# State-space part: decay products over 128 rows, per-head scalars on ScalarE, the attention half of w_out loaded beside the attention

## The chip, the cores and the metric

The kernel runs on one core of a Trainium2 chip. The metric is device time in microseconds (us) of one execution. A core has five engines with queues of their own: TensorE (PE) multiplies matrices, VectorE (DVE) and ScalarE (ACT) work on tiles from SBUF and PSUM, GpSimd (POOL) on tiles from SBUF, and SyncE (SP) issues the transfers to and from memory here. Each takes its instructions in the order in which they were written down for it; semaphores hold an instruction until what it reads is there and what it overwrites is no longer needed.

## What is computed

One encoder layer over 1024 tokens of width 1024: a half-step feed-forward network (FFN), a mixing layer, a second FFN and a gated embedding, each followed by a LayerNorm. The mixing layer has two halves: attention with 8 heads, and a bidirectional state-space scan (SSD) with 8 heads of 64 channels, 2 groups and 128 states. Their outputs, side by side, are multiplied by `w_out`. The scan is computed in chunks of 128 tokens, in both directions:

```python
a_cum = jnp.cumsum(adt, axis=-1)
seg = a_cum[..., :, None] - a_cum[..., None, :]
Lmat = jnp.exp(jnp.where(tril, seg, -jnp.inf))
cb = jnp.einsum('bclgn,bcsgn->bcgls', c_c, b_c)
y_diag = jnp.einsum('bcgls,bgrcls,bcsgrp->bclgrp', cb, Lmat, xd)
decay_states = jnp.exp(a_cum[..., -1:] - a_cum)
states = jnp.einsum('bcsgn,bgrcs,bcsgrp->bcgrpn', b_c, decay_states, xd)
...
def step(h, inp):
    st, d = inp
    return h * d[..., None, None] + st, h
...
y_off = jnp.einsum('bclgn,bcgrpn,bgrcl->bclgrp', c_c, prev, jnp.exp(a_cum))
...
y = y_f + y_b + d_skip[i].astype(jnp.float32).reshape(G, R)[:, :, None] * xh
y = y.reshape(B, S, SSD_WIDTH) * jax.nn.silu(z.astype(jnp.float32))
...
mix = jnp.concatenate([att_out, ssd_out], axis=-1) @ w_out[i]
```

## The kernel before, in words

Large products are taken in three parts: each fp32 operand is split into a high part (a cast on ScalarE, L100 `split_into`) and a low part (a subtraction on VectorE, L82 `lo`), and `mm3` (L114) sums high x low, low x high and high x high.

The order of the stages is: first FFN, projections of q, k, v, z, x, B, C and the step sizes, attention, the scan from right to left (`ssd_right`, L1160), the scan from left to right (`ssd_left`, L1230), second FFN, gate. PE runs its instructions in program order (`in_order`). On the other engines a scheduler places each instruction when the program is built, by its own estimate of times; the order that results is fixed.

`ssd_tables` (L1136) builds tables for the decay products before the attention starts: `LT` holds in 27 of 59 rows per direction three ones and three bf16 parts of eight heads' sums, `RT` (two buffers, one for even and one for odd chunks) the matching rows for the other side, `mask` the triangle, `idb` the identity.

`ssd_right` goes through chunks 7 to 0. For a chunk, `front` takes the decay matrix of each direction as products into a PSUM tile `big` (two such tiles): for each half of the heads the identity times the mask (L1183), then 27 rows of `LT` times 27 rows of `RT` (L1184). ScalarE's exponential (L1186) turns the tile into `Ef` or `Eb`. B times C goes to PSUM (L1190) and is copied to `cb` (L1192). One step later `mid` forms the skip term `y` on GpSimd (L1197), and on VectorE the sum of both directions (L1198) and its product with `cb` (L1201). `offdiag` (L1108) multiplies the running state into PSUM (L1112), scales it by head on VectorE (L1114, `toff`) and adds it to `y` on GpSimd in this pass (L1115). `next_state` (L1117) scales the chunk's input by head on GpSimd (L1120, `xs`), multiplies (L1123), scales the old state by head on GpSimd (L1128) and adds (L1129; for the first chunk L1126 copies). Two steps later `back` multiplies the decay matrix with the input (L1207), adds on VectorE (L1208) and stores `y` to `yd`. A product "by head" reads eight scalars per row, each spread over 64 columns.

Work of other kinds is put between the chunks as "fillers", called with the number of the step. In `ssd_right` these are `weights(0)` at step 1, which loads four raw tiles of the attention half of `w_out` and splits them into eight blocks `blk`, and `spilled(t)` at steps 4, 6 and 8, which multiplies one tile of 128 tokens of the attention output by it (`out_proj`, 24 matmuls of L114) and stores the result for later. In `ssd_left` they are the remaining tiles (`resident`), `weights(1)` and the tiles' second half with the LayerNorm (`mixed`).

`ssd_left` goes through chunks 0 to 7: `offdiag` (the addition on VectorE) and `next_state` for the other direction, then the product with `zs` on GpSimd (L1268), squares on ScalarE (L1272), the root on GpSimd (L128) with a correction on VectorE (L121 to L124), the scaling (L1278), and two chunks later a transpose on PE (L1251) into `mixT`, the split operand of the output projection. `mixT` takes four pairs of the buffers `xh00`, `xl00` to `xh11`, `xl11`: in each pair of halves the first number is the token half, the second 0 for the attention and 1 for the scan. Before that the same buffers held the layer's input of the projections.

## Time and profile before

| | us |
|---|---|
| median of 3 runs | 2109.38 (2101.42 to 2111.34) |
| the profiled execution | 2104.84 |
| span of its instructions | 2103.1 |
| first decay product of `ssd_right` | at 1132.91 |
| first product of `ssd_left` (L1123) | at 1208.85 |

The granted TensorE clock was 0.987 of full speed over the span. The profile gives times from the span's start. In a row of a timeline the first number is the start, the second the time taken, both in us; what stands in brackets is how long the engine had been idle and what ended that. In a row of groups the number behind `x` is the count, then total us and mean ns. The stages around the change, with the busy time of PE, weight loads, VectorE, ScalarE and GpSimd in us, then granted clock, share of the DMA engines and GB/s:

```profile
700.00:800.00 100.00, 100.00 (x474) 82.74 (x473) 56.80 (x130) 24.60 (x41) 16.35 (x9) 1.00 0.18 67
...
1050.00:1100.00 50.00, 50.00 (x302) 43.09 (x301) 46.87 (x64) 41.91 (x77) 4.87 (x6) 1.00 0.00 1
...
1200.00:1225.00 25.00, 23.76 (x107) 19.62 (x106) 9.20 (x15) 1.82 (x8) 11.04 (x10) 0.93 0.75 273
```

The first row lies in the z projection, where the tables are begun, the second in the attention, the third where `ssd_right` ends and `ssd_left` begins.

### The profile page before, as it was taken

What the parts mean: (1) busy time and instruction counts of PE and PEld (TensorE: products, weight loads), DVE (VectorE), ACT (ScalarE), POOL (GpSimd) and SP (SyncE); (2) the same over time, 40 slices, a digit from 0 to 9 for tenths busy, and PEclk for the clock granted to TensorE, in tenths of its full rate; (3) what the DMA queues carried; (4) which work ended last, traced back from release to release, by engine and by line L of the source; (5) the groups of instructions that cost most, each with busy time, mean ns of one, the idle gap of its engine ahead of it and who ended that gap; (6) DMA issues with size and microseconds to landing.
All of it is one profiled execution on the core that took longest, in us unless ns stands there. A gap on an engine that the chain in (4) does not pass through costs nothing. (4 is left out here: it accounts for less than half of the span.)

```text
span 2103.1 us, 25439 instructions
## 1 busy us (share of the span) xinstructions
PE 2024.0 (96%) x9316; PEld 1647.8 (78%) x9316; DVE 1571.8 (75%) x2339; ACT 806.1 (38%) x1324; POOL 678.4 (32%) x483
## 2 busy tenths in 40 slices
PE   7899999999999999999999998899999999999998
PEld 6688888887787888777886777688888888877886
DVE  6865665648899747658998679786666666889987
ACT  5433333335341224538886122333333334533121
POOL 0644444426530112000013542164444444541111
PEclk9999999999999999999999999999999999999999
DMA  7323433457531311220004372133333328642222
GB/s 258 114 100 121 164 116 122 149 177 273 180 111 60 117 39 37 76 74 11 1 1 144 114 270 80 71 110 122 139 130 144 128 101 323 204 133 91 71 81 80
DMA packets 94761, 254.33 MB, mean 121 GB/s; under 512 B 11585, under 2 KB 24257, under 8 KB 94636
## 3 DMA queue, kind: packets, MB, share of 16 engines
q1 hardware_dynamic: 92332, 248.51, 33.8%
q10 hardware_dynamic: 2304, 4.20, 0.5%
q8 instruction: 73, 1.20, 0.2%
q14 instruction: 52, 0.43, 0.1%
HBM read 184.84 MB, written 67.83 MB: 120 GB/s over the span
## 5 line engine op out<-in xcount | busy, mean ns | idle before, releaser
L114 PE MATMUL sm<-xh,blk 128*128 128x512 f32 x1440 | 453.5, 396 | 0.0
L114 PEld LDWEIGHTS sm<-xh,blk 128*128 128x128 f32 x1440 | 272.2, 189 | 64.7
L114 PE MATMUL sm<-xl,blk 128*128 128x512 f32 x720 | 286.2, 398 | 2.5 <-DVE xl L82 2.5
L114 PE MATMUL sm<-blk,xh 128*128 128x512 f32 (+2 forms) x912 | 277.3, 382 | 1.6 <-DVE rs_t L122 1.2
L114 PE MATMUL sm<-xl,xh 128*128 128x512 f32 x960 | 232.8, 393 | 8.0 <-DVE acc L352 7.3
L100 ACT CAST blk<-raw 128x512 fp32r<-128x512 f32 (+1 forms) x176 | 105.3, 611 | 333.6 <-PE sm L114 177.4
L114 PEld LDWEIGHTS sm<-xl,xh 128*128 128x128 f32 x960 | 178.4, 188 | 51.3 <-DVE acc L352 14.9
L82 DVE TENSOR_TENSOR blk<-raw,blk 128x512 fp32r<-128x512 f32 (+1 forms) x176 | 160.6, 923 | 58.4 <-ACT blk L100 57.7
L82 DVE TENSOR_TENSOR blk<-s,blk 128x512 fp32r<-128x512 f32 x176 | 149.0, 851 | 65.8 <-ACT blk L100 64.3
L114 PEld LDWEIGHTS sm<-blk,xh 128*128 128x128 f32 x912 | 169.7, 191 | 33.9 <-issue 1.4
L114 PE MATMUL big<-xl,xh 128*128 128x512 f32 x768 | 182.0, 394 | 6.4 <-DVE M L409 2.7
L114 PEld LDWEIGHTS big<-xl,xh 128*128 128x128 f32 x768 | 146.1, 191 | 38.2 <-ACT xl L388 5.7
L114 PE MATMUL sm<-blk,xl 128*128 128x512 f32 (+2 forms) x456 | 172.4, 378 | 0.0
L100 ACT CAST blk<-s 128x512 fp32r<-128x512 f32 x176 | 108.1, 621 | 159.9 <-PE sm L114 148.6
L114 PEld LDWEIGHTS sm<-xl,blk 128*128 128x128 f32 x720 | 136.1, 189 | 36.2 <-DVE xl L82 4.1
L244 POOL TENSOR_TENSOR s<-raw 128x512 f32<-128x512 f32 x42 | 56.0, 1332 | 291.2 <-DVE blk L82 205.8
L177 POOL TENSOR_TENSOR ln_k<-ln_k,mhalf 128x1 f32<-128x1 f32 x32 | 41.4, 1294 | 310.1 <-DVE ln_k L176 310.1
L114 PE MATMUL sm<-xET3h,blk 128*128 128x512 f32 x352 | 110.6, 395 | 0.2 <-DVE blk L82 0.2
L114 PE MATMUL sm<-xET2h,blk 128*128 128x512 f32 x352 | 110.7, 395 | 0.0
L327 POOL TENSOR_TENSOR u<-u,p 128x512 f32<-128x512 f32 x44 | 74.7, 1697 | 80.5 <-DVE u L326 80.5
L247 POOL TENSOR_TENSOR s<-raw,s 128x512 f32<-128x512 f32 x42 | 58.1, 1384 | 131.7 <-DVE blk L82 131.5
L114 PEld LDWEIGHTS sm<-blk,xl 128*128 128x128 f32 x456 | 87.2, 191 | 15.4
(303 smaller groups left out, 4046.5 us busy)
## 6 DMA issues: line engine op xcount, KB each, us to landing
raw<-in_wi_dram SPq DMA_DIRECT2D x84, 512.0 KB
hD<-sg SPq DMA_DIRECT2D x44, 512.0 KB
blk<-hD SPq DMA_DIRECT2D x44, 512.0 KB
wr<-in_wo_dram SPq DMA_DIRECT2D x32, 512.0 KB
wT<-wT SPq DMA_DIRECT2D x32, 512.0 KB
blk<-in_wo_dram SPq DMA_DIRECT2D x28, 512.0 KB
wT<-wt SPq DMA_DIRECT2D x32, 256.0 KB
wT<-wr SPq DMA_DIRECT2D x32, 256.0 KB
```

The lines of the kernel that those rows point to most:

```text
L82: (eng or self.nc.vector).tensor_tensor(out=out, in0=full, in1=hi.bitcast(F32), op=ALU.subtract)
L100: self.nc.scalar.copy(out=b[:, 0, :n], in_=src)
L114: self.nc.tensor.matmul(ps, lhsT=a, rhs=b, start=(i == 0), stop=(i == n - 1))
L177: nc.gpsimd.tensor_tensor(out=r, in0=v, in1=self.mhalf[:, :1], op=ALU.pow)
L244: G.tensor_tensor(out=s1, in0=a21, in1=a22, op=ALU.add)
L247: G.tensor_tensor(out=s4, in0=a12, in1=s2, op=ALU.subtract)
L327: G.tensor_tensor(out=u2, in0=u2, in1=p5, op=ALU.add)
```

## The change

1. The decay products take all 128 rows: `LT` becomes one zero-filled tile per direction, `RT` is zero-filled to 128 rows, and the rest of their rows stays zero, so the products are the same. The zero-fill (and the ones) moves to GpSimd; the constant rows are loaded in two halves.
2. Every GpSimd product by head (skip term, `xs`, old state) becomes eight ScalarE activations of 64 columns with a scalar per row (`scale_heads`). The addition in `offdiag` is on VectorE for both directions, and so is the product with `zs`. GpSimd keeps the roots.
3. The attention half of `w_out` is loaded in raw form into `xh01` and `xl01` right after the tables, while the attention runs, and split just before `ssd_right`. `mixT` gets its scan halves only after that, when the raw tiles have been read. The raw ring is no longer used for this half.
4. The three spilled tiles move from steps 4, 6 and 8 to steps 0, 1 and 8.

```diff
+    def scale_heads(self, out, src, small):
+
+        for h in range(8):
+            o = slice(h * HD, (h + 1) * HD)
+            self.nc.scalar.activation(out=out[:, o], in_=src[:, o], func=AF.Identity, scale=small[:, h:h + 1])
+
     def offdiag(self, pool, state, d, ch, bc, y):
...
-        (nc.gpsimd if d else nc.vector).tensor_tensor(out=y, in0=y, in1=t_, op=ALU.add)
+        nc.vector.tensor_tensor(out=y, in0=y, in1=t_, op=ALU.add)
 
     def next_state(self, pool, state, d, ch, xb):
...
-        G.tensor_tensor(out=self.heads(xs), in0=self.heads(xb[:, :512]), in1=self.per_head(self.sdt[:, ch, d * 8:d * 8 + 8]), op=ALU.mult)
+        self.scale_heads(xs, xb, self.sdt[:, ch, d * 8:d * 8 + 8])
...
-            G.tensor_tensor(out=self.heads(new), in0=self.heads(state), in1=self.per_head(self.cd[:, ch, d * 8:d * 8 + 8]), op=ALU.mult)
+            self.scale_heads(new, state, self.cd[:, ch, d * 8:d * 8 + 8])
...
     def ssd_tables(self, pool):
...
-        self.LT = LT = pool.tile([59, NT, P], BF16, name="LT")
-        self.RT = [pool.tile([59, 8, P], BF16, name=f"RT{b}") for b in range(2)]
+        self.LT = LT = [pool.tile([P, NT, P], BF16, name=f"LT{d}") for d in range(2)]
+        self.RT = [pool.tile([P, 8, P], BF16, name=f"RT{b}") for b in range(2)]
...
-        V.memset(LT, 1.0)
         for d in range(2):
+            G.memset(LT[d], 0.0)
+            G.memset(LT[d][32 * d:32 * d + 3], 1.0)
...
         for b in range(2):
-            V.tensor_copy(self.RT[1 - b], rraw)
+            G.memset(self.RT[b], 0.0)
+        for n in range(2):
+            hs = slice(4 * n, 4 * n + 4)
+            rraw = pool.tile([59, 4, P], F32, name="rraw")
+            nc.sync.dma_start(out=rraw, in_=I["rows"][:, hs])
+            for b in range(2):
+                V.tensor_copy(self.RT[b][:59, hs], rraw)
...
-                    nc.tensor.matmul(o, lhsT=LT[32 * d:32 * d + 27, ch], rhs=rt[32 * d:32 * d + 27, n * 4:n * 4 + 4], start=False, stop=True)
+                    nc.tensor.matmul(o, lhsT=LT[d][:, ch], rhs=rt[:, n * 4:n * 4 + 4], start=False, stop=True)
...
-            G.tensor_tensor(out=self.heads(y), in0=self.heads(xb[:, :512]), in1=self.per_head(dsk), op=ALU.mult)
+            self.scale_heads(y, xb, dsk)
...
-            G.tensor_tensor(out=y, in0=y, in1=zs, op=ALU.mult)
+            V.tensor_tensor(out=y, in0=y, in1=zs, op=ALU.mult)
...
-            mixT = self.new_xT()
             self.ssd_tables(tables)
+            early = []
+            for n in ("xh01", "xl01"):
+                r = self.xp.tile([P, 4, 512], F32, name=n).rearrange("p (a b) c -> p a (b c)", b=2)
+                for i in range(2):
+                    nc.sync.dma_start(out=r[:, i], in_=I["wm"][len(early)])
+                    early.append(r[:, i])
+            mixT = [[self.unit(h, 0)] for h in range(2)]
             with ExitStack() as c2:
                 self.attention(c2, mixT)
...
-            wm[half].extend(self.wload(I["wm"][half * 4 + k]) for k in range(4))
+            if half:
+                wm[1].extend(self.wload(I["wm"][4 + k]) for k in range(4))
+            else:
+                wm[0].extend([self.split(r[:, i * 512:(i + 1) * 512]) for i in range(2)] for r in early)
...
-            self.ssd_right(c, loaded, {1: lambda: weights(0), 4: lambda: spilled(0), 6: lambda: spilled(1), 8: lambda: spilled(2)})
+            weights(0)
+            for h in range(2):
+                mixT[h].append(self.unit(h, 1))
+            self.ssd_right(c, loaded, {i: lambda t=t: spilled(t) for t, i in enumerate((0, 1, 8))})
```

How the instructions stand now. ScalarE at the start of the right pass, from its last copy of the attention (`a_tmp`) on, before (`blk<-raw` is a split of w_out, `Ef` and `Eb` the exponentials, `cb` the copy of B times C):

```order
L1056 COPY a_tmp<-sm 64x512 x2
L1186 ACTIVATE Ef<-big 128x1024
L100 CAST blk<-raw 128x512
L1186 ACTIVATE Eb<-big 128x1024
L100 CAST blk<-raw 128x512
L1186 ACTIVATE Ef<-big 128x1024
L100 CAST blk<-raw 128x512 x2
L1186 ACTIVATE Eb<-big 128x1024
L1192 COPY cb<-sm 128x256 x2
```

And in the change (`y<-xb,dsk` is the skip term, `xs` the scaled input):

```order
L1056 COPY a_tmp<-sm 64x512 x2
L100 CAST blk<-xh_7569 128x512 x4
L100 CAST blk<-xl_7572 128x512 x4
L1200 ACTIVATE Ef<-big 128x1024
L1200 ACTIVATE Eb<-big 128x1024
L1206 COPY cb<-sm 128x256
L1112 ACTIVATE y<-xb,dsk 128x64 x8
L1112 ACTIVATE xs<-xb,sdt 128x64 x8
L1112 ACTIVATE y<-xb,dsk 128x64 x8
L1112 ACTIVATE xs<-xb,sdt 128x64 x4
L1200 ACTIVATE Ef<-big 128x1024
```

All eight splits now stand ahead of the first exponential, and the products by head stand between the exponentials.

ScalarE at the end of the right pass, before (`ysq` are the squares of the left pass):

```order
L1186 ACTIVATE Ef<-big 128x1024
L1186 ACTIVATE Eb<-big 128x1024
L1192 COPY cb<-sm 128x256
L1272 ACTIVATE ysq,yss<-y_10110 128x256 x2
L1272 ACTIVATE ysq,yss<-y_10114 128x256 x2
```

And in the change, from the next to last state of the pass to the left pass's first squares:

```order
L1112 ACTIVATE state<-state,cd 128x64 x8
L1112 ACTIVATE y<-xb,dsk 128x64 x5
L1112 ACTIVATE xs<-xb,sdt 128x64 x7
L1112 ACTIVATE state<-state,cd 128x64 x8
L1200 ACTIVATE Ef<-big 128x1024
L1112 ACTIVATE y<-xb,dsk 128x64 x8
L1200 ACTIVATE Eb<-big 128x1024
L1206 COPY cb<-sm 128x256
L1112 ACTIVATE xs<-xb,sdt 128x64 x24
L1112 ACTIVATE state<-state,cd 128x64 x8
L1112 ACTIVATE xs<-xb,sdt 128x64 x8
L1286 ACTIVATE ysq,yss<-y_10265 128x256 x2
```

The last state product of the right pass stands ahead of the last two exponentials; forty products by head of the left pass stand ahead of its first squares.

VectorE at the start of the right pass in the change (`a_raw` is the attention's output, `accr` the spilled tile):

```order
L1057 TENSOR_TENSOR a_raw<-sm,a_tmp 64x512 x2
L82 TENSOR_TENSOR blk<-xh_7569,blk 128x512
L1072 TENSOR_TENSOR a_raw<-a_raw,sm 128x512
L82 TENSOR_TENSOR blk<-xh_7569,blk 128x512 x3
L82 TENSOR_TENSOR blk<-xl_7572,blk 128x512 x4
L1212 TENSOR_TENSOR Eb<-Eb,Ef 128x1024
L1215 TENSOR_TENSOR Eb<-Eb,cb 128x512 x2
L1307 SCALAR_TENSOR_TENSOR accr<-sm,accr 128x512 x2
L1132 COPY state<-sm 128x512
```

There the sum of the two directions stood between the splits before; now the splits come first, and the first spilled tile's additions ahead of the first state.

More of the change, by code (lines that the diff above doesn't have):

```diff
@@ L1114, in offdiag @@
         nc.vector.tensor_tensor(out=self.heads(t_), in0=self.heads(po), in1=self.per_head(self.eF[:, ch, d * 8:d * 8 + 8]), op=ALU.mult)
[L1115 removed]
+        nc.vector.tensor_tensor(out=y, in0=y, in1=t_, op=ALU.add)
     def next_state(self, pool, state, d, ch, xb):
[L1118 removed]
+        nc = self.nc
         xs = pool.tile([P, 512], F32, name="xs")
[L1120 removed]
+        self.scale_heads(xs, xb, self.sdt[:, ch, d * 8:d * 8 + 8])
         pS = self.pss()
@@ L1138, in ssd_tables @@
         nc, I, V = self.nc, self.I, self.nc.vector
-        self.LT = LT = pool.tile([59, NT, P], BF16, name="LT")
-        self.RT = [pool.tile([59, 8, P], BF16, name=f"RT{b}") for b in range(2)]
+        G = nc.gpsimd
+        self.LT = LT = [pool.tile([P, NT, P], BF16, name=f"LT{d}") for d in range(2)]
+        self.RT = [pool.tile([P, 8, P], BF16, name=f"RT{b}") for b in range(2)]
         self.mask = pool.tile([P, 2, P], BF16, name="mask")
         self.idb = pool.tile([P, P], BF16, name="idb")
-        rraw = pool.tile([59, 8, P], F32, name="rraw")
-        nc.sync.dma_start(out=rraw, in_=I["rows"])
         mraw = pool.tile([P, 2, P], F32, name="mraw")
         nc.sync.dma_start(out=mraw, in_=I["mask"])
-        V.memset(LT, 1.0)
         for d in range(2):
+            G.memset(LT[d], 0.0)
+            G.memset(LT[d][32 * d:32 * d + 3], 1.0)
             for i in range(3):
-                nc.sync.dma_start(out=LT[32 * d + 3 + 8 * i:32 * d + 11 + 8 * i], in_=self.sc[1][d, i].rearrange("c h l -> h c l"))
+                nc.sync.dma_start(out=LT[d][32 * d + 3 + 8 * i:32 * d + 11 + 8 * i], in_=self.sc[1][d, i].rearrange("c h l -> h c l"))
         for b in range(2):
-            V.tensor_copy(self.RT[1 - b], rraw)
+            G.memset(self.RT[b], 0.0)
[5 more added lines that the diff above has]
+                V.tensor_copy(self.RT[b][:59, hs], rraw)
+        for b in range(2):
             self.rows(NT - 1 - b)
@@ L1162, in ssd_right @@
         nc, tc = self.nc, self.tc
-        V, G = nc.vector, nc.gpsimd
+        V = nc.vector
         ep = c.enter_context(tc.tile_pool(name="sexp", bufs=2))
@@ L1232, in ssd_left @@
         nc, tc = self.nc, self.tc
-        V, G = nc.vector, nc.gpsimd
+        V = nc.vector
         two = c.enter_context(tc.tile_pool(name="lwork", bufs=2))
```

1 line of the change is left out of this document (removed).

## The prediction

> **What bounds the kernel now.** I read the page first, then a table of stretches around the changed stages, then TensorE's timeline there, then the groups of the other engines.
>
> ```profile
> PE 2024.0 (96%) x9316; PEld 1647.8 (78%) x9316; DVE 1571.8 (75%) x2339; ACT 806.1 (38%) x1324; POOL 678.4 (32%) x483
> ```
>
> TensorE (PE) is busy 96% of the span.
>
> ```profile
> 1125.00:1150.00 25.00, 20.04 (x91) 12.34 (x89) 18.87 (x21) 14.39 (x25) 14.56 (x12) 0.89 0.78 255
> ...
> 1175.00:1200.00 25.00, 25.00 (x144) 19.34 (x142) 18.00 (x21) 5.65 (x8) 10.46 (x8) 1.00 0.24 82
> ...
> 1250.00:1275.00 25.00, 23.37 (x108) 18.98 (x107) 23.09 (x52) 6.56 (x19) 9.83 (x9) 1.00 0.43 148
> 1275.00:1300.00 25.00, 21.19 (x99) 17.29 (x98) 23.57 (x55) 4.42 (x10) 7.03 (x6) 0.93 0.16 63
> ```
>
> In these rows the columns after the length are busy us of PE, weight loads, VectorE (DVE), ScalarE (ACT), GpSimd (POOL), then the granted clock. The right-to-left pass (1133 to 1208) is bound by PE once it runs; ScalarE does 5.65 of 25 us there. The left-to-right pass and the start of the second FFN, up to 1356, share the bound between PE and VectorE, which is busy 92 to 94% from 1250 to 1300.
>
> ```profile
> 1132.22 0.58 ACT L1056 COPY a_tmp<-sm 64x512 f32<-64x512 f32 x1 [3.10 <-PE sm L1050]
> ...
> 1132.91 0.38 PE L1183 MATMUL big<-mask,idb 128*128 128x512 bf16 x1
> ...
> 1148.29 2.04 PE L1112 MATMUL sm<-state,bc 128*128 128x256 f32 x4 [4.82 <-DVE state L1126]
> ...
> 1153.32 0.38 PE L1183 MATMUL big<-mask,idb 128*128 128x512 bf16 x1
> ...
> 1155.86 0.71 PE L1190 MATMUL sm<-bc 128*128 128x128 f32 x4
> 1156.41 1.03 PE L1112 MATMUL sm<-state,bc 128*128 128x256 f32 x4
> 1157.27 1.03 PE L1123 MATMUL sm<-xs,xb 128*128 128x256 f32 x4
> 1158.13 1.90 PE L1207 MATMUL sm<-xb,Eb 128*128 128x64 f32 x16
> 1159.87 0.38 PE L1183 MATMUL big<-mask,idb 128*128 128x512 bf16 x1
> ...
> 1166.39 0.48 PE L114 MATMUL sm<-blk,xh 128*128 128x512 f32 x1
> ...
> 1172.08 0.39 PE L1183 MATMUL big<-mask,idb 128*128 128x512 bf16 x1
> ...
> 1208.85 1.62 PE L1123 MATMUL sm<-xs,xb 128*128 128x256 f32 x4 [1.24 <-POOL xs L1120]
> ...
> 1229.13 0.41 PE L1251 MATMUL sm<-ident,y 128*128 128x128 f32 x2 [2.95 <-DVE y L1278]
> ...
> 1281.44 1.09 PE L1251 MATMUL sm<-ident,y 128*128 128x128 f32 x4 [3.81 <-DVE y L1278]
> ```
>
> One chunk of the right pass takes PE 6.55 us (1153.32 to 1159.87): decay products 2.54, the rest 0.55, 0.86, 0.86 and 1.74. One tile of the attention half of the output projection takes 5.69 (1166.39 to 1172.08). The pass, from the first decay product at 1132.91 to the left pass's first product at 1208.85, is 75.9 us with two real waits: 4.82 for the first state, late behind the splits of w_out on VectorE, and 1.24 for `xs` on GpSimd.
>
> **The decay products over 128 rows.**
>
> ```profile
> PEld L1184 <- issue: 7.9, 32, 0.4
> PEld L1183 <- issue: 6.1, 26, 0.3
> ...
> 1166.94 0.63 PE L114 MATMUL sm<-blk,xh 128*128 128x512 f32 x2
> 1167.40 0.40 PE L114 MATMUL sm<-blk,xl 128*128 128x512 f32 x1
> ```
>
> A decay matmul starts 0.32 us after the one before (2.54/8), a 512-wide matmul of L114 0.23 (two in 0.46). The weight loads of the former wait out the running matmul; the 128-row loads of L114 do not. If the 27 rows cause it, 64 matmuls save 64 x 0.09 = 5.8 us of PE time; if the bf16 load does, nothing. I take 5.8: L1183 has 128 rows and waits too, but always behind a 27-row matmul, and L114 is the nearest row with 128 throughout. A chunk then takes PE 8 x 0.23 + 4.01 = 5.85, and the pass 8 x (1.84 + 0.55) + 14 x 0.86 + 8 x 1.74 + 3 x 5.69 = 62.1 (67.9 with nothing saved). The Trainium skill's page "TensorE: Matmul & The Clock Gate" (Part 3, The mechanism) says that a weight load overlaps running matmuls only where the row groups differ, by which full rows on both sides would save nothing. The L114 rows overlap in full rows, so the trace speaks against it; by that rule PE's 67.9 would move the start of the left pass found below from 1201.0 to 1202.3, and the sum from -10 to -9.
>
> **Scalars per head on ScalarE.** Each of 21 GpSimd products of the right pass (8 of `y`, 7 of `xs`, 6 of `state`) becomes eight activations of 128x64. No such shape is in the trace. Nearest rows:
>
> ```profile
> L1272 ACT ACTIVATE ysq<-y 128x256 f32<-128x256 f32 x16 | 6.5, 409 | 50.0 <-POOL y L1268 50.0
> ...
> L1186 ACT ACTIVATE Ef<-big 128x1024 f32<-128x1024 f32 x8 | 8.2, 1024 | 34.1 <-PE big L1184 34.1
> ...
> L1192 ACT COPY cb<-sm 128x256 f32<-128x256 f32 x8 | 2.8, 372 | 0.0
> ...
> 1104.52 1.13 ACT L1021 ACTIVATE pr<-big,nm 128x1024 f32<-128x1024 f32 x1
> 1105.53 0.21 ACT L1021 ACTIVATION_READ_ACCUMULATOR pr<-big,nm 128x1 f32 x1
> ...
> 1138.69 1.14 ACT L100 CAST blk<-raw 128x512 fp32r<-128x512 f32 x2
> ```
>
> 256 columns take 0.41, two casts of 512 take 1.14 with a length near 0.62 each, so a step of 0.52: 0.83 ns a column, and 0.10 of each operation overlaps the next. 64 columns are then 0.25 long; a per-row scalar adds 0.11 (1.13 against 1.02 for 1024 columns). Length 0.35, step 0.24 to 0.25; from the 1024-wide row with its scalar (step 1.01) the same way 0.21. Bounds: 0.21 and, with no overlap, 0.35. I take 0.24, so 1.92 us a set.
>
> ScalarE's work for a chunk becomes 2 x 0.92 (exponentials) + 0.27 (`cb`) + 24 x 0.24 = 7.9 us, more than PE's 5.85: ScalarE sets the pace of this pass. In the new order nothing there waits long for PE: splits, exponentials and products follow each other. From the end of the last attention copy at 1132.80: 8 splits x 0.52 = 4.2, 16 exponentials x 0.92 = 14.7, 8 `cb` x 0.27 = 2.2, 168 x 0.24 = 40.3; 61.4, so the last `cb` ends at 1194.2. The last state set stands ahead of two exponentials, one set and `cb` (4.0), so it ends at 1190.2; VectorE's addition makes 1191.0. From there PE is the path again: 0.86 + 1.74 + the third spilled tile 5.69 + 1.74 = 10.0, and the left pass's first product starts at 1201.0 instead of 1208.85: **-7.9**. The two exposed waits are in this, and so is the place of the spilled tiles: two now run while ScalarE works up its queue, the third covers the last exponential.
>
> **Early loading.** Four 512 KB loads leave the crowded 1125 to 1150 (0.78 of the DMA engines, above) for the end of the input projection and the attention. The splits then wait for no load; they stand at the head of ScalarE's and VectorE's queues, so the first spilled tile waits about 1.5 us for VectorE's eight halves. ScalarE's sum covers that; were PE the bound, it would cost 1.5.
>
> **VectorE and GpSimd.**
>
> ```profile
> L1201 DVE TENSOR_TENSOR Eb<-Eb,cb 128x512 f32<-128x512 f32 x16 | 18.4, 1190 | 0.0
> ...
> L1114 DVE TENSOR_TENSOR toff<-sm,eF 128x512 f32<-128x512 f32 x7 | 4.8, 681 | 0.0
> ...
> L1278 DVE SCALAR_TENSOR_TENSOR y<-y,yr,snorm 128x256 f32<-128x256 f32 x16 | 8.2, 551 | 0.0
> ...
> L1115 DVE TENSOR_TENSOR y<-y,toff 128x512 f32<-128x512 f32 x7 | 6.0, 856 | 0.6 <-DMA y<-yd 0.6
> ...
> L121 DVE TENSOR_TENSOR rs_t<-yr 128x2 f32<-128x2 f32 x8 | 3.2, 398 | 3.5 <-POOL yr L128 3.5
> ...
> L122 DVE TENSOR_TENSOR rs_t<-rs_t,yss 128x2 f32<-128x2 f32 x8 | 1.2, 148 | 0.1
> ...
> L1268 POOL TENSOR_TENSOR y<-y,zs 128x512 f32<-128x512 f32 x8 | 11.3, 1414 | 17.9 <-issue 7.8 <-DMA zs<-zd 4.8 <-PE sm L114 4.6
> ```
>
> VectorE gains 7 additions (right) and 8 products with `zs` (left), 0.6 each. It loses the stretching that GpSimd causes: with both inputs in SBUF the 512-wide operation takes 1.19 against 0.68 from PSUM. In the right pass VectorE needs some 5 us a chunk and stays covered by ScalarE's 7.9. In the left pass 8 x 0.6 = 4.8 is added and the excess of L1278, L1115 and L121 goes (16 x 0.08, 7 x 0.17, 8 x 0.25 against L122: 4.5), so about 0. The chain behind `y` gets shorter (1.41 to 0.68 a chunk, and the root on GpSimd has no queue ahead), against ScalarE's 4 us of products a chunk queued ahead of its squares. PE's waits for `y` (2.95 and 3.81) bound that gain at 6.8, the added 4.8 on VectorE bounds the loss. I take **-2.5**, nearer to nothing, because VectorE is nearly full from 1250 on.
>
> **The clock.**
>
> ```profile
> 1145.00:1150.00 5.00, 1.71 (x4) 0.50 0.47 177
> 1209.00:1213.00 4.00, 4.00 (x11) 0.57 0.82 261
> ```
>
> After the waits of 4.82 and 1.24 PE got half its clock for a while: 2.04 for four matmuls that take 1.03. With ScalarE as the bound PE idles some 2 us in each 7.9. A chunk that loses 1.7 to a slow stretch takes 7.6, still inside 7.9, so only the stretch at the end counts: +1.7. It replaces the one at 1209 that goes: 0. The Trainium skill's same page (Why this matters for your kernels) sees a lower clock only after gaps of over about 3 us, by which the new gaps would cost nothing and rival 4 below would fall away. The row after 1.24 us disagrees, and the measurement decides.
>
> The tables' new memsets, conversions and narrower loads fall where PE has no idle time (VectorE and GpSimd have some), at nothing; if a late load held VectorE by 6 us more, the four-deep results of the z part cover most of it.
>
> **Sum:** -7.9 - 2.5 = about -10. Span 2103.1 to 2093; the profiled execution took 2104.84, so 2095; the median of the runs shown is 4.5 higher, so 2099. What a measurement can tell from no change is 0.5%, 10.5 us.
>
> **Rivals.**
> 1. ScalarE hardly binds: with a step of 0.21 its sum ends 168 x 0.03 = 5.0 earlier, at PE's own limit of 1132.9 + 62.1 + 1.5 = 1196.5; that is -12.4, and with 4.5 of the waits for `y` -17: 2092. For it: the 1024-wide row; against it: the 256-wide row and any wait of ScalarE for PE.
> 2. The left pass gives it back: it starts 8 us earlier and ends where VectorE's work and the loads let it end, since VectorE is 94% busy at 1275: 2107. Against it: its work starts earlier too.
> 3. Slower: the short activations do not overlap. Each then takes its whole 0.35; the path gets 168 x 0.11 = 18.5 longer, and the left pass's 104 activations add 11 to ScalarE, of which some 3 reach the squares and so `y`: -10 + 18.5 + 3, 2121. It decides from a step of 0.30, where the gain is gone. Against it: every pair of ScalarE rows above overlaps.
> 4. The clock halves so often that ScalarE waits for PE's decay products: 1.7 in each of six chunks, 2109.
> 5. That the decay products stay at 0.32 is a way in which the change doesn't do what it says: PE's chunk is 6.55, and the 67.9 above makes it 2100.
>
> **Chances.** Forecast, with 5, 0.38 (own range 2093 to 2105); rival 1 0.18, 2 0.16, 3 0.22, 4 0.06. Faster by over 0.5% (under 2098.8): 0.18 of the forecast, 0.17 of rival 1, 0.02 of 2: 0.37. Slower (over 2119.9): 0.17 of rival 3, 0.01 each of 2 and 4: 0.19. Same: 0.44. The range runs from 2088 (PE's limit, all 6.8 of the waits and 1.7 of clock: -20.9) to 2118, where the step is 0.34 (16.8 more, and 2.7 of the 3 us at `y`).
>
> **What would show it.** Steps of the 128x64 activations near 0.24, ScalarE over 90% busy and PE's clock below 1 from 1150 to 1190, decay matmuls 0.23 apart, L1215's 512-wide products at 0.68, the left pass's first product near 1201. Wrong would be PE busy throughout the pass, or the gain gone by 1356.

## The result and the profile after

The changed kernel takes 2095.33 us (median of 10 executions, 2089.63 to 2099.91) against 2106.08 (10 executions of the kernel before beside it): ratio 0.9947, 95% interval 0.9929 to 0.9964. A second set of 9 executions gave 2091.05 and the same ratio, 0.9947 (0.9928 to 0.9965). That is 11 us less, where 10 were forecast; both intervals lie wholly under 1.

The page and the table of stretches of the changed kernel, in the same columns as before:

```profile
PE 2019.0 (96%) x9312; PEld 1645.8 (79%) x9316; DVE 1563.6 (75%) x2355; ACT 870.1 (42%) x1596; POOL 617.3 (29%) x440
```

```profile
1125.00:1150.00 25.00, 22.79 (x99) 16.45 (x99) 15.55 (x21) 21.49 (x68) 2.62 (x2) 0.93 0.47 166
1150.00:1175.00 25.00, 22.72 (x143) 18.35 (x144) 18.43 (x26) 24.14 (x78) 0.00 (x0) 1.00 0.43 134
1175.00:1200.00 25.00, 22.39 (x133) 18.05 (x132) 16.53 (x25) 17.29 (x62) 0.00 (x0) 1.00 0.25 87
...
1275.00:1300.00 25.00, 24.27 (x132) 20.32 (x131) 23.25 (x45) 8.45 (x18) 3.05 (x3) 1.00 0.16 64
```

ScalarE is busy 24.14 of the 25 us from 1150 to 1175 (5.90 before), GpSimd does nothing there, and TensorE, which had 25.00, now has 22.72: the bound of the right pass has gone from TensorE to ScalarE. ScalarE's timeline from the last attention copy to the end of the pass:

```profile
1128.16 0.58 ACT L1056 COPY a_tmp<-sm 64x512 f32<-64x512 f32 x1 [3.11 <-PE sm L1050]
...
1135.01 2.03 ACT L1112 ACTIVATE y<-xb,dsk 128x64 f32<-128x64 f32 x8
1136.94 2.02 ACT L1112 ACTIVATE xs<-xb,sdt 128x64 f32<-128x64 f32 x8
...
1185.45 2.03 ACT L1112 ACTIVATE state<-state,cd 128x64 f32<-128x64 f32 x8
1187.36 1.03 ACT L1200 ACTIVATE Ef<-big 128x1024 f32<-128x1024 f32 x1
...
1191.08 0.38 ACT L1206 COPY cb<-sm 128x256 f32<-128x256 f32 x1
1199.18 1.06 ACT L1112 ACTIVATE xs<-xb,sdt 128x64 f32<-128x64 f32 x4 [7.71 <-PE sm L1221]
```

A set of eight starts 1.93 after the set before it, so a step of 0.241. From the end of the attention's copy (1128.75) to the end of the last `cb` (1191.46) there are 62.7 us, with no wait over 0.41 in them. TensorE's timeline over the same part and the left pass:

```profile
1155.39 0.38 PE L1197 MATMUL big<-mask,idb 128*128 128x512 bf16 x1
...
1157.12 0.61 PE L1204 MATMUL sm<-bc 128*128 128x128 f32 x4
...
1171.40 1.13 PE L1118 MATMUL sm<-state,bc 128*128 128x256 f32 x4 [1.74 <-DVE state L1135]
...
1191.51 0.50 PE L114 MATMUL sm<-blk,xh 128*128 128x512 f32 x1 [0.39 <-ACT cb L1206]
...
1200.29 0.70 PE L1129 MATMUL sm<-xs,xb 128*128 128x256 f32 x2 [1.20 <-ACT xs L1112]
...
1236.16 0.83 PE L1265 MATMUL sm<-ident,y 128*128 128x128 f32 x4 [2.50 <-DVE y L1292]
...
1269.08 0.74 PE L1265 MATMUL sm<-ident,y 128*128 128x128 f32 x4 [3.25 <-DVE y L1292]
```

Eight decay products now take 1.73 us (1155.39 to 1157.12), 0.216 each against 0.32. The wait of 4.82 for the first state is gone; in its place stand three waits for VectorE's halves of the splits (0.57, 1.33 and 0.25), short waits for the state through ScalarE's queue (the longest is 1.74), 0.39 for the last `cb`, and 1.20 for the left pass's first `xs`. ScalarE could start that `xs` only when the last products with `Eb` had ended on TensorE: it had waited 7.71 for them.

Two stretches carry the comparison from here on. The **right stretch** runs from the end of the last attention copy on ScalarE to the left pass's first product: 1132.80 to 1208.85 before, 76.05; 1128.75 to 1200.29 after, 71.54. The **left stretch** runs from there to the second FFN's first product with `xET2l`: 147.56 before, 143.26 after. Together the stage went from 223.6 to 214.8 in these two executions. The attention itself ended 4.1 earlier in the execution shown of the change than in the one shown of before. I leave it out of the comparison: over all the profiled executions below it ends between 1124.2 and 1132.8, and the one of before is the latest of all. Whether some of it belongs to the change is not settled: the four kernels with the tables of before lie at 1129.9 on average, the ten with those of the change at 1127.4, and the two groups overlap.

### The profile page after: what moved, and what is told of

Read it like the earlier page. It is cut to its first block, busy times and chain, and to the rows that moved or that the text cites. A ratio compares the mean times of both kernels' runs of the same rounds, so it can differ in the third digit from the quotient of the medians.

```text
span 2095.6 us, 25632 instructions
## 1 busy us (share of the span) xinstructions
PE 2019.0 (96%) x9312; PEld 1645.8 (79%) x9316; DVE 1563.6 (75%) x2355; ACT 870.1 (42%) x1596; POOL 617.3 (29%) x440
## 4 chain that ended last, share of the span: by engine, by line
PE 80%; DVE 11%; ACT 3%; DMA 2%; issue 2%; POOL 1%; SPq 0%; DVEq 0%; ACTq 0%; POOLq 0%
PE sm L114 60%; PE big L114 9%; PE big L1012 3%; PE sm L1034 3%; DVE blk L82 2%; PE sm L1049 1%; PE sm L1050 1%; DVE xl L82 1%; DVE acc L403 1%; DVE M L409 1%; DVE M L415 1%; PE big L202 1%; DMA sg<-in_wi_dram 1%; DVE acc L352 0%; DVE xh L82 0%
## 5 line engine op out<-in xcount | busy, mean ns | idle before, releaser
L100 ACT CAST blk<-raw 128x512 fp32r<-128x512 f32 (+1 forms) x168 | 100.7, 612 | 327.2 <-PE sm L114 179.8
L82 DVE TENSOR_TENSOR blk<-raw,blk 128x512 fp32r<-128x512 f32 (+1 forms) x168 | 151.1, 910 | 56.2 <-ACT blk L100 55.3
```

Source lines behind the costliest of these rows:

```text
L82: (eng or self.nc.vector).tensor_tensor(out=out, in0=full, in1=hi.bitcast(F32), op=ALU.subtract)
L100: self.nc.scalar.copy(out=b[:, 0, :n], in_=src)
```

## The experiments

The change has three parts. I took each alone (on the kernel before) and each away (from the change), then moved single products between engines.

| kernel | time, ratio to before | right stretch | slow-clock stretches in it | left stretch |
|---|---|---|---|---|
| before | 1 | 76.05 | 2 | 147.56 |
| decay products alone | 0.9985 (0.9970 to 1.0000) | 74.49 | 3 | 146.98 |
| ScalarE part alone | 0.9990 (0.9974 to 1.0007) | 80.87 | 4 | 140.66 |
| early loads alone | 0.9997 (0.9982 to 1.0013) | 76.52 | 2 | 147.73 |
| change without ScalarE part | 0.9973 (0.9958 to 0.9988) | 71.76 | 2 | 147.83 |
| change without decay products | 0.9981 (0.9967 to 0.9996) | 79.08 | 2 | 143.06 |
| change without early loads | 0.9955 (0.9939 to 0.9972) | 75.60 | 2 | 139.13 |
| change | 0.9947 (0.9929 to 0.9964) | 71.54 | 1 | 143.26 |
| change, second execution | 0.9947 (0.9928 to 0.9965) | 70.14 | 0 | 141.57 |
| change, `y` on GpSimd | 0.9946 (0.9929 to 0.9963) | 75.94 | 5 | 138.71 |
| change, `y` twice on ScalarE | 1.0020 (1.0010 to 1.0029) | 86.16 | 5 | 141.95 |
| change, product with `zs` on GpSimd | 0.9967 (0.9953 to 0.9982) | 69.98 | 0 | 145.38 |
| change, own tile for first `xs` | 0.9945 (0.9925 to 0.9964) | 72.09 | 2 | 145.87 |
| both: own tile, `y` on GpSimd | 0.9953 (0.9938 to 0.9969) | 68.28 | 2 | 142.82 |

A slow-clock stretch is 3.41 us at half of TensorE's clock; where TensorE is the bound it costs 1.7. So a single profile tells a difference of 1 or 2 us only where their number is the same or TensorE was waiting in them.

**The decay products alone.**

```diff
-                    nc.tensor.matmul(o, lhsT=LT[32 * d:32 * d + 27, ch], rhs=rt[32 * d:32 * d + 27, n * 4:n * 4 + 4], start=False, stop=True)
+                    nc.tensor.matmul(o, lhsT=LT[d][:, ch], rhs=rt[:, n * 4:n * 4 + 4], start=False, stop=True)
```

The tables, zero-fills and narrower loads of the change go with it.

> The kernel before with the decay products over 128 rows alone (tables, masks and narrower loads of the change; scalars on GpSimd and the loads of w_out as before). Stretch meant here: from the end of the last attention copy on ScalarE to the left pass's first product; 76.05 us before, 71.55 after. Theory (TensorE bounds the right pass of the kernel before): decay matmuls 0.22 to 0.23 apart, 64 x 0.09 = 5.8 us less TensorE work, so the stretch is 70 to 71 and the time about 0.25% lower. Rival (GpSimd and VectorE are right behind TensorE there): the matmuls are as fast, but TensorE waits for xs, state or Eb take their place; stretch 74 to 76, time unchanged.

The stretch fell by 1.6, not by 5 to 6. TensorE's timeline shows what took the place of the time saved:

```profile
1132.97 0.38 PE L1191 MATMUL big<-mask,idb 128*128 128x512 bf16 x1 [1.21 <-ACT Eb L1194]
1135.66 1.13 PE L1123 MATMUL sm<-xs,xb 128*128 128x256 f32 x4 [1.22 <-POOL xs L1120]
1143.83 2.05 PE L1112 MATMUL sm<-state,bc 128*128 128x256 f32 x4 [4.55 <-DVE state L1126]
```

Two new waits, 1.21 and 1.22, and a third slow stretch (1.7) are 4.1. The products themselves are as fast as in the change. Both theories were half right: the work is saved, and a good part of it is waited for.

**The ScalarE part alone.**

```diff
-        G.tensor_tensor(out=self.heads(xs), in0=self.heads(xb[:, :512]), in1=self.per_head(self.sdt[:, ch, d * 8:d * 8 + 8]), op=ALU.mult)
+        self.scale_heads(xs, xb, self.sdt[:, ch, d * 8:d * 8 + 8])
...
-            G.tensor_tensor(out=y, in0=y, in1=zs, op=ALU.mult)
+            V.tensor_tensor(out=y, in0=y, in1=zs, op=ALU.mult)
```

(all three products per head, the right pass's addition and the product with `zs`.)

> The kernel before with the per-head scalars on ScalarE and the additions and the product with zs on VectorE alone. Theory (ScalarE sets the pace with 24 activations of 0.24 a chunk, 7.9 us a chunk): the stretch is bound by the same ScalarE sum as in the change, 62.8 from the attention's end to the last cb, plus whatever ScalarE waits for the late loads of w_out; 72 to 75. The left pass keeps its gain (the stretch from the left pass's first product to the start of the second FFN's third group, before 3.7 us longer than after, is 2 to 4 us shorter than before). Time 0.2 to 0.35% lower. Rival (the gain of the change comes from the two other parts): stretch 76 or more, time unchanged or higher.

The right stretch got longer by 4.8 and the left one shorter by 6.9. Its first set of `xs` stands in ScalarE's queue behind four splits of `w_out`, four exponentials and a set of `y`, TensorE has no spilled tile to fill the time with, and from within that wait on the clock is at half for four stretches running (one row of TensorE's timeline, one of the table of stretches):

```profile
1140.16 2.13 PE L1132 MATMUL sm<-xs,xb 128*128 128x256 f32 x4 [4.75 <-issue]
```

```profile
1137.00:1151.00 14.00, 10.84 (x27) 5.73 (x27) 8.01 (x12) 13.59 (x48) 0.00 (x0) 0.51 0.42 149
```

ScalarE is busy 13.59 of these 14 us, so the wait that the releaser column calls "issue" is for ScalarE's queue. In the right pass the rival held, in the left pass more than the theory's gain came.

**The early loads alone.** (The four loads beside the attention, as in the change, go with these lines.)

```diff
-            self.ssd_right(c, loaded, {1: lambda: weights(0), 4: lambda: spilled(0), 6: lambda: spilled(1), 8: lambda: spilled(2)})
+            weights(0)
+            for h in range(2):
+                mixT[h].append(self.unit(h, 1))
+            self.ssd_right(c, loaded, {i: lambda t=t: spilled(t) for t, i in enumerate((0, 1, 8))})
```

> The kernel before with the attention half of w_out loaded beside the attention alone, its splits at the head of the right pass and the three spilled tiles at steps 0, 1 and 8. Theory: the wait of 4.82 for the first state behind the late splits goes and with it the slow clock after it (1.7), against about 1.5 for the splits ahead of the first spilled tile: stretch 70 to 72, time 0.2% lower. Rival (GpSimd was late for the first state as well, or the spilled tiles at 0 and 1 no longer cover anything later): stretch 75 to 77, time unchanged.

The rival held. The wait of 4.82 does go, but the first spilled tile now waits for VectorE's halves of the splits, for nearly as long, and the slow clock comes with that wait too:

```profile
1135.93 0.50 PE L114 MATMUL sm<-blk,xh 128*128 128x512 f32 x1 [2.11 <-DVE blk L82]
1138.83 0.80 PE L114 MATMUL sm<-blk,xh 128*128 128x512 f32 x1 [1.93 <-DVE blk L82]
```

**The change without its ScalarE part.** The scalars, the right pass's addition and the product with `zs` go back to GpSimd (the ScalarE part's lines above, reversed).

> The change without its ScalarE part: scalars per head, the addition of the right pass and the product with zs on GpSimd again; 128-row decay products and early loads kept. Theory (ScalarE sets the pace of the right pass after the change): TensorE takes over at 5.85 a chunk, its sum 62.1 + 1.5; stretch 64 to 67 against 71.55, and the left pass gives back the 2 to 4 us that it had gained: time within 0.15% of the change's. Rival (GpSimd cannot keep 5.85 a chunk, with VectorE stretched beside it): stretch 70 to 74, time 0.1 to 0.3% above the change's.

The right stretch is 71.76, as with ScalarE; the left one gives the whole gain back (147.83). The time is in the rival's range, though not for the rival's reason in mid-pass: there TensorE is the bound again, and ScalarE's exponentials, which wait for it, come 5.63 apart.

```profile
1157.48 1.02 ACT L1200 ACTIVATE Ef<-big 128x1024 f32<-128x1024 f32 x1 [3.43 <-PE big L1198]
1163.11 1.02 ACT L1200 ACTIVATE Ef<-big 128x1024 f32<-128x1024 f32 x1 [3.43 <-PE big L1198]
```

The time is lost at the head. Groups of VectorE in the right pass, first of this kernel, then of the change:

```profile
L1215 DVE TENSOR_TENSOR Eb<-Eb,cb 128x512 f32<-128x512 f32 x16 | 20.0, 1287 | 0.1
...
L82 DVE TENSOR_TENSOR blk<-xl,blk 128x512 fp32r<-128x512 f32 x4 | 5.9, 1526 | 0.0
```

```profile
L1215 DVE TENSOR_TENSOR Eb<-Eb,cb 128x512 f32<-128x512 f32 x14 | 9.0, 688 | 0.5
...
L82 DVE TENSOR_TENSOR blk<-xl,blk 128x512 fp32r<-128x512 f32 x4 | 2.5, 680 | 0.0
```

With GpSimd's products beside them the splits take 1.53 against 0.68, TensorE waits 4.7 for them instead of 2.2, and its clock is at half for 6.8 us from the middle of that on. So in the right pass ScalarE does not beat GpSimd; it ties, under another bound.

**The change without the 128-row products.** The tables and the 27-row products of before.

> The change with the 27-row decay products and the tables of the kernel before; ScalarE part and early loads kept. Right stretch: from the end of the last attention copy to the left pass's first product (76.05 before, 71.54 after). Left stretch: from there to the second FFN's first product with xET2l (147.56 before, 143.26 after). Theory (ScalarE sets the pace of the right pass, 7.9 a chunk against TensorE's 6.55): right stretch 72 to 73.5, left stretch unchanged at 142 to 144, time within 0.1% of the change. Rival (TensorE binds as much as ScalarE, since the two alternate): right stretch 75 to 78, time 0.2 to 0.3% above the change.

79.08: past the rival's range, and 0.34% above the change where my theory had 0.1. ScalarE's queue shows why; at its end the last state set stands here behind two exponentials, `cb`, and products of `xs` and `y`:

```profile
1185.29 1.01 ACT L1192 ACTIVATE Ef<-big 128x1024 f32<-128x1024 f32 x1
...
1187.81 0.37 ACT L1198 COPY cb<-sm 128x256 f32<-128x256 f32 x1
1188.06 0.84 ACT L1112 ACTIVATE xs<-xb,sdt 128x64 f32<-128x64 f32 x3
1188.79 1.07 ACT L1112 ACTIVATE y<-xb,dsk 128x64 f32<-128x64 f32 x4
1189.74 2.02 ACT L1112 ACTIVATE state<-state,cd 128x64 f32<-128x64 f32 x8
```

In the change it stands ahead of them (1185.45 above, `Ef` only at 1187.36). It ends 62.8 after the attention against 58.7, a delay of 4.1. TensorE then waits 2.09 for the state, and two slow stretches stand in the tail (3.4 at 1.7 each); the delay and the clock together are the 7.5. The order of this queue moved with the products' length, though no line of ScalarE's work differs.

**The change without the early loads.** The fillers and loads of before.

> The change with the attention half of w_out loaded in the right pass again and its splits and spilled tiles at the steps of before (1, 4, 6, 8); ScalarE part and 128-row products kept. Theory (the early load matters once ScalarE is the long queue: late splits stand in it, and the spilled tiles at steps 0 and 1 fill TensorE while ScalarE works up its queue): right stretch 77 to 81, as with the ScalarE part alone (80.87), left stretch 140 to 144, time 0.2 to 0.4% above the change. Rival (the decay products alone make the ScalarE part pay): right stretch 72 to 75, time within 0.15% of the change.

The right stretch is 4 longer, the left one 4 shorter, and the time 0.08% above the change. The time is the rival's; the right stretch, 75.6, lies between the rival's 75 and the theory's 77. The early loads are worth little once the two other parts are in.

**One of three products off ScalarE, and one product twice on it.** These two ask whether ScalarE's sum sets the pace.

```diff
-            self.scale_heads(y, xb, dsk)
+            self.nc.gpsimd.tensor_tensor(out=self.heads(y), in0=self.heads(xb[:, :512]), in1=self.per_head(dsk), op=ALU.mult)
```

> The change with one of its three per-head products, y, on GpSimd again (8 of 21 sets of the right pass; xs and state stay on ScalarE, all additions on VectorE). Theory (ScalarE's 7.9 a chunk sets the pace): ScalarE's chunk falls to 6.0, its sum by 15.4, and TensorE's own limit takes over (62.1, some 2 for the splits, 1.7 for a slow stretch of the clock, 1.3 for xs): right stretch 67 to 69, left stretch unchanged at 143, time 0.1 to 0.2% below the change. Rival (another chain, state through VectorE and the splits at the head, is as long): right stretch 70 to 72, time that of the change.

```diff
             self.scale_heads(y, xb, dsk)
+            self.scale_heads(y, xb, dsk)
```

> The change with the product y of the right pass made twice on ScalarE (the second time over the first, same values): 64 more activations, 15.4 us of ScalarE work. Theory (ScalarE's sum sets the right pass of the change): right stretch, slow stretches of the clock taken off at 1.7 each, 15 us above the change's 69.8: 84 to 86; left stretch unchanged. Rival (TensorE, the splits and VectorE's part of the chain to the state set it, ScalarE is only nearly as long): 5 to 12 us above.

With `y` twice the stretch is 86.16, 14.6 above the change for 15.4 of work, and the ratio is 0.73% above the change's, also 15.4 us. By the letter of the expectation, with the five slow stretches taken off, it is 77.6 and would be the rival's; but that subtraction is wrong where TensorE has time to spare. The rows tell it apart (the pass as one window, and two of the waits of TensorE that are new):

```profile
1129.00:1200.00 71.00, 58.29 (x280) 42.48 (x277) 41.89 (x57) 70.89 (x244) 2.62 (x2) 0.88 0.31 103
```

```profile
1159.66 0.99 PE L1129 MATMUL sm<-xs,xb 128*128 128x256 f32 x2 [3.07 <-ACT xs L1112]
...
1188.55 1.22 PE L1129 MATMUL sm<-xs,xb 128*128 128x256 f32 x2 [3.98 <-ACT xs L1112]
```

ScalarE is busy 70.89 of 71 us and TensorE idle 12.7, so what TensorE's clock does there lengthens nothing: ScalarE's sum sets the pass. With `y` on GpSimd the other side shows. ScalarE now waits for TensorE, and TensorE's stretch without its slow clock is 67.4 (75.94 less five times 1.7), where the theory had 67 to 69 with one slow stretch in it:

```profile
1148.14 1.02 ACT L1200 ACTIVATE Ef<-big 128x1024 f32<-128x1024 f32 x1 [6.71 <-PE big L1198]
```

```profile
1190.00:1202.00 12.00, 10.88 (x36) 9.32 (x37) 5.34 (x9) 0.00 (x0) 0.00 (x0) 0.57 0.19 66
```

But as the bound TensorE also pays for the slow clock, here three stretches running at the end, and the time is that of the change (0.9946), as the rival had it, though the rival's stretch of 70 to 72 was missed as well. The clock is not low in this one execution alone: on average over its 6 executions 0.9873 of full speed was granted, against 0.9897 and 0.9909 in the two sets of the change. More ScalarE work costs its full length; `y` given back to GpSimd brings nothing that can be measured: the change stands near the point where the two engines meet.

**The product with `zs` back on GpSimd** (the last two lines of the ScalarE part, reversed).

> The change with the left pass's product with zs on GpSimd again and all else kept. Theory (the left pass gains from the shorter chain to y: the product takes 0.68 on VectorE against 1.41 and a queue on GpSimd): right stretch unchanged at 71.5, left stretch back to 146 to 148. Rival (the gain of the left pass is GpSimd's xs and state products gone, which had stretched VectorE's operations): left stretch 142 to 144.

The left stretch is 145.38, 2.1 to 3.8 above the two executions of the change, and the time 0.2% above: by these figures about half of the left pass's gain is this one product. Neither figure is clear of chance (the difference of the ratios is known to 0.23%), and 145.38 lies between the theory's 146 and the rival's 144. The rows are clear. It is not only the product's own length. Groups of the left pass from 1200 to 1300, of this kernel, then of the change:

```profile
L1282 POOL TENSOR_TENSOR y<-y,zs 128x512 f32<-128x512 f32 x8 | 10.6, 1327 | 108.9 <-DMA y<-yd 75.7 <-DVE y L1121 13.7 <-DVE ln_k L157 10.5
L1292 DVE SCALAR_TENSOR_TENSOR y<-y,yr,snorm 128x256 f32<-128x256 f32 x16 | 9.0, 606 | 0.1
```

```profile
L1292 DVE SCALAR_TENSOR_TENSOR y<-y,yr,snorm 128x256 f32<-128x256 f32 x16 | 7.0, 482 | 0.2
...
L1282 DVE TENSOR_TENSOR y<-y,zs 128x512 f32<-128x512 f32 x8 | 5.5, 686 | 0.0
...
L121 DVE TENSOR_TENSOR rs_t<-yr 128x2 f32<-128x2 f32 x8 | 1.2, 148 | 0.8 <-POOL yr L128 0.8
```

1.33 becomes 0.69, and L1292 falls from 0.61 to 0.48.

**An own tile for the left pass's first `xs`, alone and with `y` on GpSimd.**

```diff
-        xs = pool.tile([P, 512], F32, name="xs")
+        xs = self.xs0 if d == 0 and state is None else pool.tile([P, 512], F32, name="xs")
```

> The change with the first xs of the left pass in a tile of its own in the pool of the tables, not in the pool opened after the right pass. In the change this product waits 7.71 on ScalarE for TensorE's last products with Eb, and TensorE then waits 1.20 and 0.25 for it. Theory (the wait is for memory that the right pass still reads): both waits and, in part, the slow clock at 1201.6 go: right stretch 1.2 to 1.5 shorter (without slow stretches 68.3 to 68.6), left stretch 0 to 2 shorter. Rival (the product waits for something else, the chunk or its table): no change.

> Both: the product y on GpSimd, and the first xs of the left pass in a tile of its own. Theory (the gains add, since one is the pace of the pass and the other its end): right stretch without slow stretches 66 to 66.5 (67.4 with y on GpSimd alone), left stretch 137 to 139; time 0.1 to 0.25% below the change. Rival (the clock takes it back: less waiting for ScalarE brings more slow stretches, as with y on GpSimd alone, where five stand in the right pass): time that of the change.

The wait at the left pass's first product goes in both, so it was for memory that the right pass still read. Without their slow stretches the right stretches are 68.7 (68.3 to 68.6 expected) and 64.9 (66 to 66.5 expected). The left stretches missed: 145.87 alone, where 0 to 2 less than the change's 143.26 was expected, and 142.82 with both, where 137 to 139 was. Alone the own tile shortened the stage by nothing: the first chunk's `y` is then late instead.

```profile
1220.64 1.11 PE L1266 MATMUL sm<-ident,y 128*128 128x128 f32 x4 [3.73 <-DVE y L1293]
```

Both together have the shortest stage of all (68.28 + 142.82), 0.6 below the better execution of the change, and a ratio of 0.9953: no version here is measurably faster than the change.

**The change once more.**

> The change itself once more, to see how far its stretches move from one profiled execution to the next. Right stretch 70 to 72 if ScalarE sets it (71.54 in the first, 69.98 in the run that differs from it in the left pass alone), left stretch 141 to 145, time 0.4 to 0.65% below the kernel before. Rival (the stretches vary by two or more slow stretches of the clock, 3.4 us, from one execution to the next): right stretch 73 or more, or left outside 140 to 146; then differences of that size between single profiles say nothing.

70.14 and 141.57: the right stretch moves by 1.4 where ScalarE sets it, the stage as a whole by 3.1. Differences of 2 or 3 us between single profiles are therefore not told from chance here, and I draw on those only where the medians or the waits say the same.

## Why the prediction was right

**The sum.** -10 was forecast; the stage shows -8.8 and -11.9 in two executions, the medians about -11. That the sum came out so near is in part luck. The split between the passes was off: -7.9 forecast and -4.5 to -5.9 found in the right pass, -2.5 forecast and -4.3 to -6.0 found in the left. The right pass fell short, and the clock, which stood at 0 in the sum, made up for it (below). That the left pass's first product came at 1200.3, where 1201.0 had been forecast, is in part chance: the attention ended 4.1 earlier in that execution.

**ScalarE as the bound.** This was the main step, and it held in its own terms: step 0.24 forecast and 0.241 measured, length 0.35 and 0.35, and its sum 61.4 against 62.7 (1.2 of it waits) and, in the second execution, 61.3. The Trainium skill's page "ScalarE: Activation LUTs" (What ACT_TABLE_LOAD costs) would have given the same: 186 ns and 0.833 per column, 93 more for a pointer operand and 93 of overlap, an estimate of 0.33 and 0.24 for 64 columns; the trace agrees, with 0.35 and 0.241. The run with `y` twice shows that this sum sets the pass; rivals 1 (hardly binds) and 3 (no overlap) fall.

**The tail.** The right stretch was forecast at 68.2 (1132.8 to 1201.0) and took 71.5. Of these 3.3, 1.3 lie in ScalarE's sum up to the last state set (57.4 forecast, 58.7 found; 57.3 in the second execution) and 2.0 behind it, in both executions, the term that I mis-sized: I had VectorE's addition and 10.0 of TensorE's work there, 10.8 together, and found 12.8. The additional pieces are 0.39 for the last `cb` ahead of the third spilled tile, 1.20 for the left pass's `xs`, and 0.4 of pipeline ends that a wait exposes. The 1.24 that I counted as removed came back with ScalarE in GpSimd's place.

**The decay products.** Step 0.23 forecast, 0.216 measured, with full rows on both sides: the 27 rows had caused the 0.32. But I had them off the path, with 67.9 instead of 62.1 to cost only 1.3 (rival 5). Taking them out costs 7 us (0.34%, known to 0.23). Where two engines hand work to each other within each chunk, the second one's length is not free below the first one's: the run without them shows the order of ScalarE's queue change with it. Over the four pairs of runs that differ in one part alone the ratios give, on average, 0.27% for the decay products, 0.21% for the ScalarE part and 0.08% for the early loads (each to about 0.11: 0.16 for a ratio, times the root of 8, over 4), together 0.56%. So the decay products are at least as large a part of the gain as the scalars, not one of no effect; which of the two is larger is not told.

**The early loads.** That the splits "then wait for no load" was right and worth little: the wait for the state turned into waits for VectorE's halves of the splits, some 2 us together in the change and 4 to 4.7 where GpSimd works beside VectorE; I had 1.5. The forecast said that ScalarE's sum covers that, and in the change it does.

**The left pass.** The mechanism held: the chain to `y` is shorter, and VectorE is no longer stretched (L1292 0.48 against 0.55, L121 0.148 against 0.398, the addition of `toff` 0.68 against 0.86; 121.8 us of work in the stretch against 123.3, with eight products more). TensorE waits 5.75 for `y` instead of 7.4 (the 6.8 of the forecast lacks a wait of 0.68), and 17.3 in all instead of 20.3. The rest of the 4.3 and 6.0 is about one slow stretch less in the first execution and two in the second.

**The clock** was wrong. I forecast a granted clock under 1 through the ScalarE-bound part; the row from 1150 to 1200 says 1.00, with waits of up to 1.74 in it. Rival 4 falls with it. And the sum had the clock at nothing, where it is a good part of the gain. In the stage stand 8 slow stretches before, 6 and 4 in the two executions of the change. With half of TensorE's busy time in them taken off (an estimate of what they cost), the right stretch is 74.5 before and 69.8 and 70.1 after, the left one 138.7 before and 136.5 and 136.6 after: 4.4 to 4.7 gained where 7.9 was forecast, and 2.1 to 2.2 where 2.5 was. Nor is that chance alone: the clock granted over whole executions is 0.9870 to 0.9874 on average in the four sets of the kernel before (14 to 35 executions each), and 0.9897 and 0.9909 in the two sets of the change (10 and 9), so up to 5.0 and 7.6 us of the 11, the share of the clock that is no longer withheld, are clock. Without the ScalarE part it is 0.9873 again (12 executions). Why the kernel with ScalarE as the bound loses less of it was not looked for.

**Rival 2** (given back later) has a grain of truth. From the second FFN's first product with `xET2l` to the start of the 150th matmul after it TensorE takes 37.9 us in both executions of the change and 34.9 before, so 3.0 is given back. In it are two waits that the kernel before does not have, 1.34 and 0.45 (0.49 in the second execution). The first is for an addition on VectorE (L330) that stands behind VectorE's splits; the second is for L329, which waits for GpSimd:

```profile
1361.03 3.48 DVE L82 TENSOR_TENSOR blk<-raw,blk 128x512 fp32r<-128x512 f32 x2
1364.43 0.68 DVE L330 TENSOR_TENSOR sg<-u,sm 128x512 f32<-128x512 f32 x1
1365.26 0.47 PE L114 MATMUL sm<-xET3l,blk 128*128 128x512 f32 x1 [1.34 <-DVE sg L330]
...
1379.19 0.69 DVE L329 TENSOR_TENSOR u<-u,sm 128x512 f32<-128x512 f32 x1 [2.43 <-POOL p L328]
```

So the account of the 11 us is about this: 6.5 to 6.8 of work and waits in the stage, less 3.0 given back, and 5.0 to 7.6 of clock, together 8.5 to 11.4.

What stays open is whether the parts help each other: alone they give 0.15, 0.10 and 0.03%, together 0.53%, but each ratio is known only to 0.16%, so the excess is not clear of chance.

## What to carry to other kernels

Before work is moved to an idle engine, add up that engine's whole queue over the stage and set it against the engine that bounds the stage now: the pass ends with the longer sum, and here the place where the two meet was the best one found: more on ScalarE cost its full length, `y` off it brought nothing. An engine just under the bound is not free, since the order and the handing over within each chunk turn its length into waits. And an engine that stretches another's operations is worth emptying even where it is not the bound: VectorE's products with both inputs in SBUF took 0.69 instead of 1.29 once GpSimd was still. And read the granted clock over all executions before a gain is put down to work saved: here up to 5.0 or 7.6 us of 11 were clock.

## What the hardware showed that I had not expected

The half-clock stretches do not follow the length of a wait. Each lasts 3.41 us, and within one execution all of them up to 2060 us start on one grid: their distances are whole multiples of 3.413 us, to 2 ns, while the grid lies elsewhere in the next execution. What goes with them is how busy TensorE was in the stretch of the grid just before. In the 14 profiles, from 20 to 2060 us, 138 slow stretches follow one at full clock; TensorE was busy at most 0.70 of the 3.41 us ahead of each, and no stretch with more was followed by one (7863 at full clock). All 94 with less than 0.41 were. Between the two both happen. So the same waits can cost a stretch or not: those of 1.20 and 0.25 at the start of the left pass fell into one stretch of the grid in the first execution of the change, and its edge lay between them in the second (length, then TensorE's busy time first and the granted clock behind the engines, first execution, then second):

```profile
1198.11:1201.52 3.41, 1.95 (x12) 1.42 (x12) 0.69 (x1) 2.34 (x10) 0.00 (x0) 1.00 0.59 231
1201.52:1204.94 3.42, 3.42 (x9) 2.68 (x9) 0.69 (x1) 3.42 (x16) 0.00 (x0) 0.50 0.88 234
```

```profile
1192.64:1196.06 3.42, 2.69 (x21) 2.37 (x19) 1.63 (x3) 0.64 (x3) 0.00 (x0) 1.00 0.47 186
1196.06:1199.47 3.41, 2.68 (x11) 1.96 (x12) 0.69 (x1) 3.41 (x15) 0.00 (x0) 1.00 0.75 219
1199.47:1202.88 3.41, 3.41 (x16) 2.78 (x15) 0.69 (x1) 3.41 (x16) 0.00 (x0) 1.00 0.99 312
```

Why a slow stretch is sometimes followed by more is open: three came running around a wait of 1.46 and four around one of 4.75, the last of them with TensorE at work throughout. The Trainium skill's page "TensorE: Matmul & The Clock Gate" (What's actually happening) speaks of a free-running window of activity, which agrees with the fixed length and the grid; no run here shows what exactly it counts. Up to 2060 us 9 to 18 slow stretches stood in these profiles; nine more would cost 15 us, an estimate at 1.7 each, if all of them fell on TensorE's path.

TensorE's step for 512-wide products has two values: the mean time from one start to the next is 232.4 or 233.3 ns throughout an FFN, chosen anew for the first and the second, whatever the kernel (of 14 profiles 4 have the slower one in the first FFN and 4 in the second, one of them in both). From 1400 to 1760 us that is 1.5 us more. Its cause was not looked for.
